# Row maximum over 16,384 rows of 1,024 floats: eight rows per partition moved to TensorE and GpSimd, fewer and larger loads, a later first store

## Chip, cores, metric

One core of a Trainium2 chip. The metric is the device time of one execution in microseconds (us). Engines in the profile: PE is TensorE (PEld its weight loads), DVE is VectorE, ACT is ScalarE, POOL is GpSimd, SP issues the loads.

## The reference

```python
x = np.random.randn(32, 512, 1024).astype(np.float32)
def reference(x):
    return np.max(x, axis=-1).astype(np.float32)
```

64 MiB are read (67.11 MB), 64 KB written. With 128 partitions that is 128 rows of 4,096 B per partition.

## The kernel before

Rows are taken in two blocks. In a block each partition owns neighbouring rows, so a load of g rows is one run of g x 4,096 B per partition. A ring of 46 rows per partition holds them; VectorE reduces each load as it lands; each block's maxima are stored when it is done.

```python
BLOCKS = [
    [14, 14, 12, 11, 9, 8, 8, 7, 6, 5, 4, 4, 4, 3, 3],
    [2, 2, 2, 2, 2, 1, 1, 1, 1, 1, 1],
]
RING = 46
# ... cut ...
        for g in loads:
            if at + g > RING:
                at = 0
            xc = ring[:, at:at + g, :]
            nc.sync.dma_start(out=xc, in_=xb[:, b:b + g, :])
            nc.vector.reduce_max(out=res[:, first + b:first + b + g], in_=xc, axis=X)
            at += g
            b += g
        # ... dst: this block's part of the output ...
        nc.scalar.dma_start(out=dst, in_=res[:, first:first + S])
```

Of the kernel before, what the change touches and what calls it, by code (L numbers as in the profile page):

```python
# [1 line left out]

# [4 lines left out]


F32 = mybir.dt.float32



BLOCKS = [
    [14, 14, 12, 11, 9, 8, 8, 7, 6, 5, 4, 4, 4, 3, 3],
    [2, 2, 2, 2, 2, 1, 1, 1, 1, 1, 1],
]
RING = 46


@with_exitstack  # L20
def kernel(
    ctx: ExitStack,
    tc: tile.TileContext,
    x: bass.AP,
    out: bass.AP,
):
    nc = tc.nc
    P = 128
    X = mybir.AxisListType.X

    xf = x.flatten_outer_dims()
    N, D = xf.shape
    I = N // P
    of = out.flatten_outer_dims()

    once = ctx.enter_context(tc.tile_pool(name="once", bufs=1))
    ring = once.tile([P, RING, D], F32)
    res = once.tile([P, I], F32)

    at = first = 0  # L40
    for loads in BLOCKS:
        S = sum(loads)
        xb = xf[first * P:(first + S) * P, :].rearrange("(p i) d -> p i d", p=P)
        b = 0
        for g in loads:
            if at + g > RING:
                at = 0
            xc = ring[:, at:at + g, :]
            nc.sync.dma_start(out=xc, in_=xb[:, b:b + g, :])  # L49
            nc.vector.reduce_max(out=res[:, first + b:first + b + g], in_=xc, axis=X)  # L50
            at += g
            b += g
        dst = bass.AP(tensor=of.tensor, offset=of.offset + first * P, ap=[[S, P], [1, S]])
        nc.scalar.dma_start(out=dst, in_=res[:, first:first + S])
        first += S
    assert first == I


# [1 line left out]
_INS = ['x']  # L60
_OUTS = [((32, 512), 'float32')]


# [23 lines left out]
```

## Time and profile before

| | before |
|---|---|
| time, median of 6 runs | 165.06 us (165.01 to 165.14) |
| span of the profiled run | 163.3 us |
| VectorE busy | 138.5 us |
| VectorE waiting for loads | 22.4 us, 20.1 of them for the first |
| last load landed / last reduction ended | 159.46 / 160.88 us |

### The profile page before, as it was taken

To read this page: it belongs to the slowest core of one execution; us is meant where nothing else is said; L and a number is where in the kernel's file an instruction comes from. 1 tells how busy PE (TensorE), PEld (TensorE's weight loads), DVE (VectorE), ACT (ScalarE), POOL (GpSimd) and SP (SyncE) were. 2 spreads that over 40 slices of the span, in tenths; PEclk is the share of its full clock that TensorE was granted. 3 is DMA by queue.
4 is the path that set the end of the run, shared out by engine and by line. 5 is a ranking of instruction groups with operands and counts; after the bars stand their busy time and mean duration, and the time that the engine had idled before them with its cause. 6 is when DMAs were issued, how large, how long until landed. Compare 5 with 4: busy or idle time off the path is not lost.

```text
span 163.3 us, 109 instructions
## 1 busy us (share of the span) xinstructions
DVE 138.5 (85%) x26; POOL 0.2 (0%) x4
## 2 busy tenths in 40 slices
DVE  0000099969999999999999999999999999999994
POOL 0000000000000000000000000000000000000000
DMA  6999999998899897999989999999999999999980
GB/s 225 449 449 449 449 449 449 449 417 385 385 409 522 353 530 321 433 433 441 473 385 473 425 449 400 434 395 451 413 425 433 429 414 418 425 421 419 404 357 2
DMA packets 4032, 67.18 MB, mean 411 GB/s; under 512 B 704, under 2 KB 704, under 8 KB 1472
## 3 DMA queue, kind: packets, MB, share of 16 engines
q1 hardware_dynamic: 3744, 67.11, 96.4%
q10 hardware_dynamic: 288, 0.07, 0.2%
HBM read 67.11 MB, written 0.07 MB: 411 GB/s over the span
## 4 chain that ended last, share of the span: by engine, by line
DMA 57%; DVE 40%; DVEq 1%; SPq 0%; issue 0%
DMA ring<-in_x_dram 57%; DVE res L50 40%; DVEq L82 1%; SPq L49 0%
## 5 line engine op out<-in xcount | busy, mean ns | idle before, releaser
L50 DVE TENSOR_REDUCE res<-ring 128x1 f32<-128x1024 f32 (+11 forms) x26 | 138.5, 5396 | 22.4 <-DMA ring<-in_x_dram 22.4
L71 POOL MEMSET const-bfloat16-1.0<- 128x1 bf16 x1 | 0.1, 101 | 0.0
L71 POOL MEMSET const-uint8-127<- 128x1 uint8 x1 | 0.1, 101 | 0.0
L71 POOL MEMSET const-float32-0.0<- 128x1 f32 x1 | 0.1, 98 | 0.2 <-issue 0.2
L71 POOL MEMSET const-float32-1.0<- 128x1 f32 x1 | 0.1, 98 | 0.0
## 6 DMA issues: line engine op xcount, KB each, us to landing
ring<-in_x_dram SPq DMA_DIRECT2D x2, 7168.0 KB, 27.6
ring<-in_x_dram SPq DMA_DIRECT2D x2, 4096.0 KB, 31.6
ring<-in_x_dram SPq DMA_DIRECT2D x1, 6144.0 KB, 49.9
ring<-in_x_dram SPq DMA_DIRECT2D x3, 2048.0 KB, 36.8
ring<-in_x_dram SPq DMA_DIRECT2D x1, 5632.0 KB, 29.7
ring<-in_x_dram SPq DMA_DIRECT2D x5, 1024.0 KB, 24.6
ring<-in_x_dram SPq DMA_DIRECT2D x1, 4608.0 KB, 23.7
ring<-in_x_dram SPq DMA_DIRECT2D x1, 3584.0 KB, 38.4
```

Of the source, the lines that this page charges most:

```text
L50: nc.vector.reduce_max(out=res[:, first + b:first + b + g], in_=xc, axis=X)
L71: nc = _bacc.Bacc("TRN2", target_bir_lowering=False, num_devices=1)
L82: with _tile.TileContext(nc) as tc:
```

## The change

Intent: eight rows per partition, out of loads that land after 120 us, take another way. TensorE turns the row block (eight turns, that is transpositions, of 128x128 into PSUM), ScalarE copies it to SBUF, GpSimd takes the maximum over partitions (the all-reduce), TensorE turns the result back, and VectorE only reduces eight numbers (the collection). The freed VectorE time is to pay for larger loads, which cost the DMA engines less. The last row comes in two halves. The first block's store goes behind the last load.

A load is now (rows, rows for GpSimd, load after which VectorE collects their result). Loads are numbered from 0.

```diff
 BLOCKS = [
-    [14, 14, 12, 11, 9, 8, 8, 7, 6, 5, 4, 4, 4, 3, 3],
-    [2, 2, 2, 2, 2, 1, 1, 1, 1, 1, 1],
+    [(15, 0, -1), (14, 0, -1), (14, 0, -1), (15, 0, -1), (15, 0, -1), (13, 0, -1), (12, 3, 7), (8, 1, 9), (6, 2, 12)],
+    [(4, 1, 14), (2, 0, -1), (2, 1, 17), (1, 0, -1), (1, 0, -1), (1, 0, -1), (1, 0, -1), (1, 0, -1), (1, 0, -1), (1, 0, -1)],
 ]
-RING = 46
+RING = 45
@@ cut @@
+    def by_gpsimd(rows, cols, m):
+        back = psmall.tile([P, m, C], F32)
+        for k in range(m):
+            ps = psum.tile([P, D], F32)
+            for c in range(C):
+                nc.tensor.transpose(out=ps[:, c * P:(c + 1) * P], in_=rows[:, k, c * P:(c + 1) * P], identity=ident)
+            sb = turn.tile([P, D], F32)
+            nc.scalar.copy(out=sb, in_=ps)
+            top = allr.tile([P, D], F32)
+            nc.gpsimd.partition_all_reduce(top, sb, P, bass_isa.ReduceOp.max)
+            run(backs)
+            def turn_back(top=top, k=k):
+                for c in range(C):
+                    nc.tensor.transpose(out=back[:, k, c:c + 1], in_=top[0:1, c * P:(c + 1) * P], identity=ident[0:1, 0:1])
+            backs.append(turn_back)
+        return lambda: nc.vector.reduce_max(out=cols, in_=back, axis=X)
@@ in the loop over loads @@
+            if m:
+                due.setdefault(w, []).append(by_gpsimd(xc[:, n - m:, :], cols[:, n - m:], m))
+            else:
+                run(backs)
+            if j == 0:
+                nc.gpsimd.tensor_copy(out=ident[:, 0:1], in_=xc[:, 0, 0:1])
+                make_identity(nc, ident)
+            if n > m:
+                reduce = nc.vector.reduce_max(out=cols[:, :n - m], in_=xc[:, :n - m, :], axis=X)
+            run(due.get(j, []))
@@ after the loop @@
+    nc.sync.dma_start(out=half, in_=xb[:, b, :H])
+    nc.sync.dma_start(out=tail[:, PAD:], in_=xb[:, b, H:])
+    nc.vector.reduce_max(out=tail[:, PAD - 1:PAD], in_=half, axis=X)
+    nc.vector.reduce_max(out=res[:, I - 1:], in_=tail[:, PAD - 1:], axis=X)
+    store = nc.scalar.dma_start(out=views[0][0], in_=views[0][1])
+    tc.add_manual_dep(store.ins, reduce.ins.name, SYNC, reason="behind the loads")
+    nc.scalar.dma_start(out=views[1][0], in_=views[1][1])
```

The next row is turned before the last one is turned back, and load 6's three results are collected after load 7's own rows, and so on.

More of the change, by code (lines that the diff above doesn't have):

```diff
@@ L6 @@
 from concourse._compat import with_exitstack
+from concourse import bass_isa
+from concourse.masks import make_identity
 F32 = mybir.dt.float32
 BLOCKS = [
-    [14, 14, 12, 11, 9, 8, 8, 7, 6, 5, 4, 4, 4, 3, 3],
-    [2, 2, 2, 2, 2, 1, 1, 1, 1, 1, 1],
-]
-RING = 46
+    [(15, 0, -1), (14, 0, -1), (14, 0, -1), (15, 0, -1), (15, 0, -1), (13, 0, -1), (12, 3, 7), (8, 1, 9), (6, 2, 12)],
+    [(4, 1, 14), (2, 0, -1), (2, 1, 17), (1, 0, -1), (1, 0, -1), (1, 0, -1), (1, 0, -1), (1, 0, -1), (1, 0, -1), (1, 0, -1)],
+]
+RING = 45
+SYNC = mybir.DependencyInfo(mybir.DependencyClass.Sync, mybir.DependencyReason.DATA)
 @with_exitstack
@@ L32 @@
     N, D = xf.shape
+    H = D // 2
+    C = D // P
     I = N // P
@@ L36 @@
     once = ctx.enter_context(tc.tile_pool(name="once", bufs=1))
+    turn = ctx.enter_context(tc.tile_pool(name="turn", bufs=2))
+    allr = ctx.enter_context(tc.tile_pool(name="allr", bufs=2))
+    psum = ctx.enter_context(tc.tile_pool(name="psum", bufs=3, space=bass.MemoryType.PSUM))
+    psmall = ctx.enter_context(tc.tile_pool(name="psmall", bufs=2, space=bass.MemoryType.PSUM))
     ring = once.tile([P, RING, D], F32)
     res = once.tile([P, I], F32)
-    at = first = 0
+    ident = once.tile([P, P], F32)
@@ new lines @@
+    PAD = 16
+    tail = once.tile([P, PAD + H], F32)
+    backs = []
+    due = {}
+    def by_gpsimd(rows, cols, m):
[3 more added lines that the diff above has]
+            for c in range(C):
+                nc.tensor.transpose(
+                    out=ps[:, c * P:(c + 1) * P],
+                    in_=rows[:, k, c * P:(c + 1) * P],
+                    identity=ident,
+                )
+            sb = turn.tile([P, D], F32)
[5 more added lines that the diff above has]
+                for c in range(C):
+                    nc.tensor.transpose(
+                        out=back[:, k, c:c + 1],
+                        in_=top[0:1, c * P:(c + 1) * P],
+                        identity=ident[0:1, 0:1],
+                    )
+            backs.append(turn_back)
+        return lambda: nc.vector.reduce_max(out=cols, in_=back, axis=X)
@@ L41, with run @@
+    def run(calls):
+        while calls:
+            calls.pop(0)()
+    at = first = j = 0
+    views = []
     for loads in BLOCKS:
-        S = sum(loads)
+        S = sum(n for n, m, w in loads) + (loads is BLOCKS[-1])
         xb = xf[first * P:(first + S) * P, :].rearrange("(p i) d -> p i d", p=P)
+        dst = bass.AP(tensor=of.tensor, offset=of.offset + first * P, ap=[[S, P], [1, S]])
+        views.append((dst, res[:, first:first + S]))
         b = 0
-        for g in loads:
-            if at + g > RING:
+        for n, m, w in loads:
+            if at + n > RING:
@@ L47 @@
                 at = 0
-            xc = ring[:, at:at + g, :]
-            nc.sync.dma_start(out=xc, in_=xb[:, b:b + g, :])
-            nc.vector.reduce_max(out=res[:, first + b:first + b + g], in_=xc, axis=X)
-            at += g
-            b += g
-        dst = bass.AP(tensor=of.tensor, offset=of.offset + first * P, ap=[[S, P], [1, S]])
-        nc.scalar.dma_start(out=dst, in_=res[:, first:first + S])
+            xc = ring[:, at:at + n, :]
+            nc.sync.dma_start(out=xc, in_=xb[:, b:b + n, :])
@@ new lines @@
+            cols = res[:, first + b:first + b + n]
+            if m:
[8 more added lines that the diff above has]
+            run(due.get(j, []))
@@ L55 @@
+            at += n
+            b += n
+            j += 1
         first += S
     assert first == I
+    half = ring[:, at, :H]
+    nc.sync.dma_start(out=half, in_=xb[:, b, :H])
[4 more added lines that the diff above has]
+    tc.add_manual_dep(store.ins, reduce.ins.name, SYNC, reason="behind the loads")
```

## The prediction

> **What bounds the kernel now.** I read the page first (busy shares, slices, queues), then the engine waits, the chain of waits, the groups by form, and a table of windows over the end.
>
> ```profile
> DVE 138.5 (85%) x26; POOL 0.2 (0%) x4
> ...
> DVE  0000099969999999999999999999999999999994
> ...
> DMA  6999999998899897999989999999999999999980
> ...
> q1 hardware_dynamic: 3744, 67.11, 96.4%
> ```
>
> Two resources are nearly full. The load queue q1 is busy for 96.4% of 163.3 us = 157.4 us, so 67.11 MB move at 426 GB/s; its digits have no hole. VectorE (DVE) is busy 138.5 us, and that is all of its time once data is there:
>
> ```profile
> DVE res L50 <- DMA ring<-in_x_dram: 22.4, 4, 20.1
> ```
>
> It waits 22.4 us in all, 20.1 of them for the first load. 22.4 + 138.5 = 160.9: its end. Which of the two ends the kernel is read in the last pieces of the chain and in the windows:
>
> ```profile
> 95.08 36.77 DMA ring<-in_x_dram
> 131.85 0.02 issue
> 131.87 19.94 DMA ring<-in_x_dram
> 151.81 0.02 issue
> 151.84 7.92 DVE res L50 x6
> 159.75 1.13 DVEq L82
> ```
>
> ```profile
> 120.00:155.00 35.00, 34.81 (x12) 0.00 (x0) 1.00 1.01 422
> 155.00:160.00 5.00, 5.00 (x6) 0.00 (x0) 1.00 0.76 304
> 160.00:163.30 3.30, 0.88 (x1) 0.00 (x0) 1.00 0.03 3
> ```
>
> The chain names VectorE for the last 8 us, but the windows show the loads at full share until about 159 (0.76 of 5 us = 3.8 us after 155). The semaphore records put the last landings at 158.21 and 159.46. The last reduction runs from 159.67 to 160.88: VectorE lags the final load by only 0.2 us. So the DMA stream is the bound and VectorE a co-bound that follows one row behind. Then the second store is issued at 160.91 and landed at 162.33 (1.42 us); the span closes 1.0 us later.
>
> ```profile
> L50 DVE TENSOR_REDUCE res<-ring 128x14 f32<-128x14336 f32 x2 | 30.2, 15086 | 22.0 <-DMA ring<-in_x_dram 22.0
> L50 DVE TENSOR_REDUCE res<-ring 128x2 f32<-128x2048 f32 x5 | 11.2, 2279 | 0.2 <-DMA ring<-in_x_dram 0.2
> L50 DVE TENSOR_REDUCE res<-ring 128x1 f32<-128x1024 f32 x6 | 6.8, 1208 | 0.0
> ```
>
> A row per partition costs VectorE 15,086 / 14 = 1.078 us in a long instruction. From two rows against one, 1.046 ns an element and 0.137 us fixed.
>
> The packet records of the trace (no view prints them; one packet is one partition of one load, eight to an engine) say what load size is worth: median 161 ns at 4,096 B, 309 at 8,192, 1,213 at 32,768, 2,116 at 57,344. The slope from 8 to 56 KB is 36.77 ns per KB of 1,000 B, with 7.8 ns fixed per packet (10.4 for the single rows). One row is 4,096 B, so 150.6 ns.
>
> **What the Trainium skill says.** "DMA: Bandwidth & Descriptors", section "Where 436 GB/s comes from", gives 435.2 GB/s as the ceiling of 16 engines. The trace agrees: 4,096 B / 150.6 ns x 16 = 435.2 GB/s before the fixed part. So nothing that reads all 67.11 MB gets below 154.2 us of stream.
> "GPSIMD Engine Reference", section 3.2 "Cross-partition", gives 247,699 ns for GpSimd's reduction over partitions of [128, 2048]. The change uses another instruction, the all-reduce, for which I find no duration on that page; the kernel before runs neither.
> "TensorE: Matmul & The Clock Gate", Part 4 "PE-mode transpose", has about 275 ns in context and 390 ns alone for a 128x128 bf16 turn; here the data is f32, and no run shows one yet.
> "ScalarE: Activation LUTs", section "What ACT_TABLE_LOAD costs", has 186 ns + 0.833 ns an element without pointer operands. That would make the 1,024-column copy 1.04 us, an estimate; the trace before has no ScalarE copy.
>
> **The change part by part.**
>
> *Larger loads.* 26 loads become 21 (19 plus two halves of the last row). Every row still costs 8 x 150.6 ns = 1.205 us, 154.2 in all. Fixed part before: 8 x (26 x 7.8 + 6 x 2.6) ns = 1.75 us; after: 8 x (21 x 7.8 + 9 x 2.6) = 1.50 us. Gain 0.25 us. This is why a large rearrangement can move so little. Five fewer completion packets of 9 ns per engine take 0.05 more.
>
> *First block's store moved.* It is 128 packets of 448 B at 25 ns, eight an engine: 0.20 us, now among the loads (issued at 142.87, loads end at 159). After, it is issued when the last loop load has been reduced, so most of it lies behind the stream. Gain 0.20 us of stream. It is ahead of the second store on the same issuing queue, by about 1.3 us, and its own issue takes some 0.4 us, so I give it 0.1 us of delay to the end.
>
> Last landing after: 159.46 - 0.25 - 0.05 - 0.20 = 158.96.
>
> *Tail.* The last whole row lands about two half rows earlier, at 157.7 (2 x 0.6 us). VectorE reduces it to 158.9 (pitch 1.125 us in the timeline, from 156.29 to 157.42), then the first half (512 elements, 0.67 us, pitch about 0.58) to 159.4, then the second half with the first's result as element 513, 0.67 us, to 160.1. Before it was 160.9. So the end moves 0.8 us, of which 0.5 is the landing and 0.3 the halved last reduction. With 0.1 for the two stores: 0.7 us.
>
> *Eight rows off VectorE.* 8 x 1.078 = 8.6 us of 138.5, less a handful of small PSUM reductions. It buys no time directly because the stream sets the end; it buys slack, so that VectorE can catch up before the last rows although bigger loads start it later (15 rows instead of 14 first: +1.2 us, to 21.3). 21.3 + 130 = 151.3, against a last loop row at 157.7: about 6 us of slack.
>
> *The new path.* Per row: eight turns (about 2.5 us, estimate from the skill's figures), a ScalarE copy (1.04), one GpSimd all-reduce T, eight small turns back (about 1.5). The rows are taken from loads 6, 7, 8, 9 and 11, which by 1.205 us a row land at 121.7, 131.4, 138.7, 143.6 and 148.5. VectorE collects the results after loads 7, 9, 12, 14 and 17, which I put at 139.0, 146.9, 151.8, 154.1 and 157.2. Three rows must fit in 17.3 us: 3T + 5.1 < 17.3, T < 4.1. From load 8 on four rows run one behind another to 157.2: 4T + 5.1 < 18.5, T < 3.35. The program fixes its collecting points unevenly, and these limits lie close together; I read that as fitted to a known T of about 3 us. That is an inference from the program, not from the trace. T below 3.35 costs nothing.
>
> **Rivals.**
> *GpSimd becomes the bound.* VectorE is in order, so a late collection stalls it. With T = 4 the last result comes 4 x 0.65 = 2.6 us late, and the end moves from -0.7 to about +1.9 us: 167.0. With T = 5 it is some 6 us over: 171. If the all-reduce behaved like the skill's partition reduction, 121 ns a column, 124 us a row, the kernel would take a millisecond. For: no duration in the profile. Against: the fitted collecting points.
> *The stream runs dry.* Load 4 (15 rows) reuses ring rows 15 to 30, which needs load 2's reduction: it lands at 55.2, ends at 70.3. Load 3's data lasts until about 73.0, and a load takes 1.0 us from issue (0.73) to first packet (1.73). The margin is 1.6 us, so no hole. If there is one, it is added whole: about +1 us. Elsewhere loads are queued by more than 10 us (before: at least 8.7 from issue to landing).
> *New traffic.* TensorE's instructions, and whatever GpSimd's all-reduce has to fetch, share the 16 engines with a stream that has no spare time. Each 0.1 us of it per engine is 0.1 us at the end. Likely some tenths; half of the gain could go, giving 164.7 to 165.1.
> *VectorE was the true bound*, as the chain says, and 8.6 us come off: 157 us. Against it: landing 159.46, 0.2 us before the last reduction. The ceiling forbids it.
>
> **Range and chances.** 165.07 - 0.7 = 164.4 as the main line. With 0.3 of new traffic it is 164.7, without and with a luckier tail 163.7; a late collection by 1 to 2 us makes 165.5 to 166.5. I state 164.5, range 163.6 to 166.0. Faster by 2% means under 161.8, which is less than stream 154.2 + start 1.7 + receipt and ramp 1.4 + a half-row reduction 0.7 + store and close 2.4 + 1.8 between span and time = 162.2: 0.01. Slower by 2% needs 168.4, so T above roughly 4.4 us or several troubles together: 0.08. Within 2%: 0.91.
>
> **What would show it.** Right: q1 still over 95% busy; windows from 20 to 155 at 425 to 432 GB/s; VectorE near 130 us busy with idle gaps of about 6 us in total before small loads, all named as waiting for loads; second store issued near 160.1; GpSimd all-reduces starting under 3.4 us apart. Wrong: a VectorE wait for TensorE's turned-back result among the last loads (GpSimd bound); a low DMA digit near 73 us (ring); loads slower than 1.205 us a row in the stage where GpSimd works (traffic or contention); or a span that starts its loads later than 0.73 us because of what the new engines set up.

## The result, and the profile after

181.52 us, median of 6 runs (181.04 to 182.66), against 165.06. The ratio is 1.100 (1.097 to 1.104): slower by 10%, 15.5 us above the top of the predicted range.

The page of the changed kernel:

```profile
PE 21.4 (12%) x128; PEld 19.4 (11%) x128; DVE 130.7 (73%) x26; ACT 9.4 (5%) x9; POOL 26.6 (15%) x15
...
DVE  0000299979995998499939999999963993387194
ACT  2000000000000000000000000000410222022000
POOL 0000000000000000000000000000793609370600
...
DMA  6999999999999999999999989999999999930000
...
q1 hardware_dynamic: 3024, 67.11, 87.7%
```

The loads end at slice 36 of 40, around 161 us, and the kernel goes on for 19 us. VectorE has holes where it had none, and GpSimd has holes between its bursts too: it is not full. VectorE's waits:

```profile
DVE res L115 <- DMA ring<-in_x_dram: 31.2, 6, 21.3
...
DVE res L86 <- PE back L79: 15.7, 4, 5.9
```

The balance closes: 31.2 + 15.7 + 130.7 = 177.6 us, VectorE's end, against 22.4 + 138.5 = 160.9 before. The 16.7 us more are 15.7 of waits for results turned back (L86 is the collection) and 8.8 of more waiting for loads, less 7.8 that came off as work. The first collection, in VectorE's timeline:

```profile
123.77 9.75 DVE L115 TENSOR_REDUCE res<-ring 128x9 f32<-128x9216 f32 x1 [0.18 <-DMA ring<-in_x_dram]
...
137.78 0.18 DVE L86 TENSOR_REDUCE res<-back 128x3 f32<-128x24 f32 x1 [4.26 <-PE back L79]
137.88 7.61 DVE L115 TENSOR_REDUCE res<-ring 128x7 f32<-128x7168 f32 x1
```

The three results of load 6 are collected *before* load 7's seven rows, which had landed at 133.46. The source has it the other way round. The chain of waits shows the second displacement:

```profile
133.38 3.31 POOL top L74
136.69 0.04 issue
136.74 1.01 PE back L79 x8
137.75 1.92 PE ps L66 x8
139.66 0.02 issue
...
139.74 1.02 ACT sb L72
140.76 0.08 issue
140.84 3.23 POOL top L74
```

TensorE turns row 3 back (136.74) and only then turns load 7's row (137.75), although the source writes load 7's turns first. So turn-back, turn, copy and all-reduce stand end to end: 7.4 us from one all-reduce to the next, of which the all-reduce is 3.25. The same pattern comes at 148.2, 158.8 and 166.2, and five whole rows and two halves are still to be reduced when the last result is there at 170.5.

The orders of the instructions, listed engine by engine, confirm it. The program builder puts instructions into an order of its own and does not keep that of the source. VectorE's collections stand before loads 7, 8 and 9, after load 10 and after load 13; the source says after loads 7, 9, 12, 14 and 17. TensorE finishes all turn-backs of a load before it turns a row of the next.

The durations themselves were as assumed or shorter:

```profile
L74 POOL PARTITION_ALL_REDUCE top<-sb x8 | 25.8, 3256 | 110.6 <-ACT sb L72 110.6
...
L72 ACT COPY sb<-ps 128x1024 f32<-128x1024 f32 x8 | 8.1, 1012 | 156.0 <-PE ps L66 154.3
```

Last, the stream. It ended at 160.83, where 158.96 was predicted and the kernel before had 159.46.

### The profile page after: what moved, and what is told of

Read it like the earlier page. It is cut to its first block, busy times and chain, and to the rows that moved or that the text cites. A ratio compares the mean times of both kernels' runs of the same rounds, so it can differ in the third digit from the quotient of the medians.

```text
span 180.0 us, 400 instructions
## 1 busy us (share of the span) xinstructions
PE 21.4 (12%) x128; PEld 19.4 (11%) x128; DVE 130.7 (73%) x26; ACT 9.4 (5%) x9; POOL 26.6 (15%) x15
## 4 chain that ended last, share of the span: by engine, by line
DMA 50%; DVE 22%; POOL 11%; PE 7%; issue 4%; ACT 2%; POOLq 2%; ACTq 0%; SPq 0%
DMA ring<-in_x_dram 50%; DVE res L115 21%; POOL top L74 11%; PE ps L66 4%; ACT sb L72 2%; PE back L79 2%; POOLq L158 2%; DVE res L127 0%; DVE tail L126 0%; ACTq L72 0%; DVE res L86 0%; SPq L104 0%
## 5 line engine op out<-in xcount | busy, mean ns | idle before, releaser
L115 DVE TENSOR_REDUCE res<-ring 128x1 f32<-128x1024 f32 (+8 forms) x19 | 129.0, 6827 | 31.2 <-DMA ring<-in_x_dram 31.2
L74 POOL PARTITION_ALL_REDUCE top<-sb x8 | 25.8, 3256 | 110.6 <-ACT sb L72 110.6
L66 PE MATMUL ps<-ident,ring 128*128 128x128 f32 x64 | 14.0, 405 | 123.9 <-DMA ring<-in_x_dram 123.9
L66 PEld LDWEIGHTS ps<-ident,ring 128*128 128x128 f32 x64 | 12.4, 218 | 123.9 <-issue 123.8
L72 ACT COPY sb<-ps 128x1024 f32<-128x1024 f32 x8 | 8.1, 1012 | 156.0 <-PE ps L66 154.3
L86 DVE TENSOR_REDUCE res<-back 128x1 f32<-128x8 f32 (+2 forms) x5 | 0.8, 169 | 15.7 <-PE back L79 15.7
L79 PE MATMUL back<-ident,top 1*128 1x1 f32 x64 | 7.7, 237 | 25.2 <-POOL top L74 25.2
L79 PEld LDWEIGHTS back<-ident,top 1*128 1x128 f32 x64 | 7.0, 204 | 27.1 <-POOL top L74 27.1
L127 DVE TENSOR_REDUCE res<-tail 128x1 f32<-128x513 f32 x1 | 0.7, 687 | 0.0
L126 DVE TENSOR_REDUCE tail<-ring 128x1 f32<-128x512 f32 x1 | 0.7, 679 | 0.0
```

The source lines that it names most:

```text
L66: nc.tensor.transpose(out=ps[:, c * P:(c + 1) * P], in_=rows[:, k, c * P:(c + 1) * P], identity=ident,)
L72: nc.scalar.copy(out=sb, in_=ps)
L74: nc.gpsimd.partition_all_reduce(top, sb, P, bass_isa.ReduceOp.max)
L79: nc.tensor.transpose(out=back[:, k, c:c + 1], in_=top[0:1, c * P:(c + 1) * P], identity=ident[0:1, 0:1],)
L86: return lambda: nc.vector.reduce_max(out=cols, in_=back, axis=X)
L115: reduce = nc.vector.reduce_max(out=cols[:, :n - m], in_=xc[:, :n - m, :], axis=X)
```

## The experiments

**Theory.** The compiled order on VectorE and TensorE makes the collections early and the all-reduces late. **Rival A:** the all-reduces themselves are the bound (8 x 3.25 us from 127 us on). **Rival B:** the later stream is what costs. The edits pin an instruction behind the one traced before it on its engine; by their intent they add no wait on another engine.

```diff
-                nc.tensor.transpose(
+                tc.keep_in_program_order(nc.tensor.transpose(      # both kinds of turns: "TensorE pinned"
-        return lambda: nc.vector.reduce_max(out=cols, in_=back, axis=X)
+        return lambda: tc.keep_in_program_order(nc.vector.reduce_max(out=cols, in_=back, axis=X))   # and the row reductions: "VectorE pinned"
```

### Both orders pinned

> The changed kernel with its turns on TensorE and its reductions on VectorE held to the order in which the source states them. My theory (the scheduler issued the collections one to two loads early and each row's turn-back ahead of the next row's turns, so VectorE idled 15.7 us on results): about 168.7 us. Worked out from the trace of the changed kernel: the three results of load 6 are collected at 141 with no idling, the turn-back of load 9's row still stands ahead of load 11's turns in the source, so the last result comes at about 162.0, VectorE ends near 164.4 and the store adds 2.4 and the launch 1.8. Rival A (the all-reduce's own 8 x 3.25 us is the bound): 180 or more, within 2 us of the changed kernel. Rival B (the load stream that ends 1.4 us later is what costs): at least 179.

169.44 us (169.01 to 170.24), ratio 1.027. 12 us come back from order alone, so rivals A and B fall as the main cause: both said at least 179. What is left of VectorE's waits for results is one of 3.54 us, for the last one. Its all-reduce starts at 158.58, after GpSimd has stood idle again:

```profile
DVE res L86 <- PE back L79: 3.5, 1, 3.5
...
158.58 3.22 POOL L74 PARTITION_ALL_REDUCE top<-sb  x1 [4.16 <-ACT sb L72]
```

The turn-back of load 9's row still stands ahead of load 11's turns, in the source itself.

### TensorE's order only

Both are pinned, but the collections are traced where the compiled changed kernel had them, so VectorE's order is exactly that of the changed kernel.

```diff
+            run(due.get(j, []))
             if n > m:
                 reduce = ...
-            run(due.get(j, []))
-(12, 3, 7), (8, 1, 9), (6, 2, 12)   (4, 1, 14)   (2, 1, 17)
+(12, 3, 7), (8, 1, 8), (6, 2, 9)    (4, 1, 11)   (2, 1, 14)
```

> Only TensorE in the source's order; VectorE's order pinned to exactly that of the changed kernel (early collections). My theory: about 173.2 us, since the first collection still stalls VectorE by 4.3 us before load 7, but the later all-reduces start about 4 us earlier each and later stalls shrink to 1 to 2 us. Rival A: 180 or more. If the early collections on VectorE were the whole cause: 179 to 181.

173.83 us (173.62 to 174.54), ratio 1.054.

### VectorE's order only

```diff
-                reduce = nc.vector.reduce_max(out=cols[:, :n - m], in_=xc[:, :n - m, :], axis=X)
+                reduce = tc.keep_in_program_order(nc.vector.reduce_max(out=cols[:, :n - m], in_=xc[:, :n - m, :], axis=X))   # and the collections
```

VectorE pinned alone; the compiled orders of the other four engines are then the same as in the changed kernel.

> Only VectorE in the source's order; TensorE, ScalarE and GpSimd exactly as in the changed kernel. My theory: about 177.2 us: the all-reduces keep their times (the last ends at 169.4), so the last result still comes at 170.5 and only one whole row and two halves follow it instead of five and two halves: 4 x 1.125 us gained. If the early collections on VectorE were the whole cause: about 166 to 169. Rival A: 177 as well, so this run alone does not tell A apart; the run with TensorE's order does.

176.67 us (176.28 to 177.49), ratio 1.071. The waits on collections, of the run with TensorE's order and then of this one:

```profile
DVE res L86 <- PE back L79: 8.4, 3, 5.2
```

```profile
DVE res L86 <- PE back L79: 11.0, 3, 5.0
```

Out of 15.7 us each order alone removes a part. TensorE's order is worth more by itself (7.7 us of time against 4.8), because it also brings the last result forward, from 170.5 to 163.3.

### Both orders, and the turn-back of load 9's row behind load 11's turns

```diff
-            else:
+            elif j != 10:
                 run(backs)
```

> Both orders, and in addition the turn-back of load 9's row put behind load 11's turns. My theory: 166.2 us: the last all-reduce starts at about 153.7, its result is there at 158, before load 17 is reduced (159.5), so VectorE follows the loads to the end: 160.8 for the last landing, 162.0 for the last reduction. About 2.5 us less than with both orders alone. If GpSimd had no spare time in the tail it would be no faster than with both orders alone.

166.22 us (165.63 to 166.85), ratio 1.007. VectorE no longer waits for a result, and GpSimd's eight all-reduces (3.25 us each, as before) fit. Around the first collection, in the timeline:

```profile
124.39 17.33 DVE L115 TENSOR_REDUCE res<-ring 128x9 f32<-128x9216 f32 x2 [0.20 <-DMA ring<-in_x_dram]
...
135.10 1.97 PE L66 MATMUL ps<-ident,ring 128*128 128x128 f32 x8
...
138.31 1.01 PE L79 MATMUL back<-ident,top 1*128 1x1 f32 x8 [1.25 <-POOL top L74]
...
141.64 0.17 DVE L86 TENSOR_REDUCE res<-back 128x3 f32<-128x24 f32 x1
```

Load 6 and load 7 are reduced back to back (17.33 us, x2). Load 7's turns run at 135.1, ahead of the turn-back at 138.3, and the collection at 141.6 waits for nothing. The 1.1 us that remain against the kernel before lie in the stream, as the next run tests. (The profiled execution was the slowest of the four, 166.85 us.)

### The same with loads 4 and 5 of 14 and 14 rows

Load 4 of 15 rows takes ring rows 15 to 29, of which row 29 is load 2's, so it is issued only when load 2 is reduced (71.1 us in the changed kernel). Below, the spread of a load is the time between the first and the last of its 16 completions, one per DMA engine.

```diff
-(15, 0, -1), (15, 0, -1), (13, 0, -1), (12, 3, 7)
+(15, 0, -1), (14, 0, -1), (14, 0, -1), (12, 3, 7)
```

> As the run with both orders and the late turn-back, with loads 4 and 5 of 14 and 14 rows instead of 15 and 13. Load 4 then reuses only load 1's rows of the ring and can be issued at about 54 instead of 71 us. If the late issue at 71 us is what makes the DMA engines fall apart (in that run the 16 completions of a load spread over 1.3 us for load 2 and 2.6 us for load 4): spread after load 4 about 1.3, stream end about 1 us earlier, 165.2 us. If the spread has another cause (the library that GpSimd fetches from 22 us on): no change, 166.2.

165.40 us (165.11 to 165.68), ratio 1.0017 (1.0004 to 1.0030). The step at load 4 is gone; a spread that arises between loads 0 and 2 stays (table below).

### No GpSimd path, the changed kernel's loads

```diff
-(12, 3, 7), (8, 1, 9), (6, 2, 12)   (4, 1, 14)   (2, 1, 17)
+(12, 0, -1), (8, 0, -1), (6, 0, -1)  (4, 0, -1)   (2, 0, -1)
-                nc.gpsimd.tensor_copy(...); make_identity(nc, ident)
```

> The changed kernel's loads, halves and late stores, but all rows on VectorE; no TensorE, ScalarE copy or GpSimd. My theory: the larger loads make VectorE wait for data about 10 us more before load 6 (waits of 1.2, 2.2, 3.3 and 2.9 us in the changed kernel), and without the eight rows taken off it cannot catch up: from load 6 at 123.7 it has 138.6 - 92.6 = 46 us left, ends at about 169.7, so 173.6 us. If larger loads cost nothing, as the prediction had it: about 165 to 167. The completions of a load should stay within 0.5 us of each other up to load 3 if the spread comes from GpSimd's library.

172.79 us (172.17 to 173.04), ratio 1.046.

```profile
DVE 138.4 (81%) x21; POOL 0.2 (0%) x4
```

```profile
DVE res L114 <- DMA ring<-in_x_dram: 30.5, 6, 21.4
```

30.5 + 138.4 = 168.9: VectorE alone cannot follow these loads. Their price is about 8 us more waiting than before (30.5 against 22.4), 1.3 of it for the first load and the rest between 38 and 93 us:

```profile
38.33 15.09 DVE L114 TENSOR_REDUCE res<-ring 128x14 f32<-128x14336 f32 x1 [0.76 <-DMA ring<-in_x_dram]
55.27 15.09 DVE L114 TENSOR_REDUCE res<-ring 128x14 f32<-128x14336 f32 x1 [1.85 <-DMA ring<-in_x_dram]
73.41 16.15 DVE L114 TENSOR_REDUCE res<-ring 128x15 f32<-128x15360 f32 x1 [3.05 <-DMA ring<-in_x_dram]
92.75 30.08 DVE L114 TENSOR_REDUCE res<-ring 128x15 f32<-128x15360 f32 x2 [3.19 <-DMA ring<-in_x_dram]
```

So the eight rows on the other path only buy back what the larger loads take. Of the descending sizes before, VectorE lost 1.85 us in this stretch.

### The same with loads of 14 and 14

```diff
-(15, 0, -1), (15, 0, -1), (13, 0, -1), (12, 0, -1)
+(15, 0, -1), (14, 0, -1), (14, 0, -1), (12, 0, -1)
```

> No GpSimd path and loads 4 and 5 of 14 and 14 rows. With the three runs before it this fills a square: late issue at 71 us (yes or no) by GpSimd's library (yes or no). If these two are the only causes of the spread of a load's 16 completions, it stays at 0.5 to 0.6 us from the first load to the last, and the stream ends at 159.3 or earlier. The time is set by VectorE, which has all rows: about 172.2 us.

172.37 us (172.19 to 172.46), ratio 1.044. The spread holds at 0.3 to 0.4 us, and the last load lands at 159.01.

### The same with the identity matrix on GpSimd

```diff
             if j == 0:
-                pass
+                nc.gpsimd.tensor_copy(out=ident[:, 0:1], in_=xc[:, 0, 0:1])
+                make_identity(nc, ident)
```

> The run before it plus only the identity matrix on GpSimd (a copy, a memset and the select with its one library, no all-reduce, no turns). If the libraries make the spread: about 1.1 us from load 1 on as in the run with the path, and no further step at load 2, because the all-reduce's library is not fetched. If the path's work on the rows makes it: 0.5 us, as without GpSimd. Time 172.2 to 173.

172.26 us (172.20 to 172.36), ratio 1.043. Spread 0.25 us throughout, so my expectation of 1.1 us failed. The reason is in GpSimd's timeline. Changed kernel first, then this one:

```profile
21.61 0.20 POOL masks.py:197 MEMSET ident<- 128x128 f32 x1
32.78 0.28 POOL masks.py:199 TENSOR_SCALAR_AFFINE_SELECT ident<-ident 128x128 f32<-128x128 f32 x1 [10.96 <-issue]
```

```profile
21.55 0.20 POOL masks.py:197 MEMSET ident<- 128x128 f32 x1
21.82 0.29 POOL masks.py:199 TENSOR_SCALAR_AFFINE_SELECT ident<-ident 128x128 f32<-128x128 f32 x1
```

The traces have a configuration instruction on GpSimd (MODIFY_POOL_CONFIG), which I take for the choice of the library that holds the code of what follows. In the changed kernel one stands at 21.87 us, 10.9 us before the select, and another at 33.31 for the all-reduces. Here the only one stands at 21.73, 0.09 us before the select. I read it so: with the all-reduce in the program two libraries alternate, and each execution waits 11 us for the select's; with the select alone its library is still there from the execution before. So this run clears the identity's instructions but says nothing of a fetch. The next one does.

### One library, all rows on the path

The run of 165.40 us with a small all-reduce in place of GpSimd's first copy, which makes the builder serve the select from the all-reduce's library: the trace has a configuration at 0.81 us and none at the select.

```diff
-                nc.gpsimd.tensor_copy(out=ident[:, 0:1], in_=xc[:, 0, 0:1])
+                nc.gpsimd.partition_all_reduce(ident[:, 0:8], xc[:, 0, 0:8], P, bass_isa.ReduceOp.max)
```

> The run with both orders, the late turn-back and loads of 14 and 14, except that GpSimd's first instruction after the first load is a small all-reduce of eight columns in place of the copy. The identity's select then runs from the same library as the all-reduces, so one library serves the whole program and stays from one execution to the next, as the select's did in the run with the identity only (0.09 us from configuration to select, against 10.9 in the changed kernel). If fetching libraries is what slows the loads: no 11 us gap on GpSimd after 22 us, the spread of a load's completions stays at 0.5 us with all eight rows still on the path, the stream ends at about 159.1, and the time is 164.3 us, below the kernel before (165.1). If the path's work itself makes the spread: 1.6 us of spread and 165.4 us as before.

165.72 us (165.60 to 165.84), ratio 1.004. The gap is gone (select at 22.44), and the spread does not move from 0.82 us while it rose to 1.66 in the run with two libraries. So changing libraries did cause that part: all six runs with two libraries rise by 0.5 to 1.1 us between loads 0 and 2, and none of the other runs does. (Load 0's 0.84 is the highest of all; whether something is fetched after the configuration at 0.81 does not show.) But the time did not come: between the landings at 148.95 and 151.31 the spread jumps to 1.85, and the stream ends at 160.10, no earlier. In that interval, from 149.13 on, the one packet of another queue keeps a DMA engine busy for 1.08 us:

```profile
q8 instruction: 1, 0.02, 0.0%
```

It is 16 KB of instructions. All runs with the path have it and none without. In the 165.40 us run it comes at 159.17, where little is left to delay. But in the changed kernel and in the run with VectorE's order it comes inside the stream too (154.96 and 155.16, 1.08 and 1.02 us long), and there the spread stays at 1.9 and 2.4. If the packet delays the engine that it meets, that was not the slowest one there; the records do not tell which it was.

The semaphore records give the spreads (us, one profiled execution each). A load counts only when the slowest engine is done.

| run | two libraries | load 4 issued late | load 0 | load 2 | load 4 | last load | last landing, us |
|---|---|---|---|---|---|---|---|
| before | no | no | 0.40 | 0.38 | 0.42 | 0.48 | 159.46 |
| no path, 14 and 14 | no | no | 0.43 | 0.40 | 0.41 | 0.29 | 159.01 |
| no path | no | yes | 0.56 | 0.52 | 1.53 | 1.33 | 160.09 |
| both orders, late turn-back, 14 and 14 | yes | no | 0.57 | 1.66 | 1.65 | 1.58 | 160.06 |
| both orders, late turn-back | yes | yes | 0.49 | 1.29 | 2.64 | 2.55 | 161.48 |
| changed kernel | yes | yes | 0.58 | 1.32 | 1.92 | 1.81 | 160.83 |
| one library, 14 and 14 | no | no | 0.84 | 0.83 | 0.82 | 1.65 | 160.10 |

In these pairs late issue and changed libraries each put about 1.1 us on the slowest engine (160.09 and 160.06 against 159.01). Together they put 1.6 to 2.5, by the five runs that have both. The size differs from run to run: with both orders pinned, the spread was 1.75 at load 2 and no larger at load 4 (1.72), though the last load still landed at 160.63.

### The store and the halves on the kernel before

First the store alone. My edit tied it to the very last reduction, later than the change does.

```diff
+    store = nc.scalar.dma_start(out=views[0][0], in_=views[0][1])      # behind both blocks
+    tc.add_manual_dep(store.ins, reduce.ins.name, SYNC, reason="behind the loads")
```

> The kernel before with only the first block's store moved behind the last load's reduction. Prediction's term: 0.2 us of stream, less up to 0.1 for the two stores in a row: 164.9 to 165.0. If the two stores in one queue cost more than the stream gains: 165.1 to 165.4.

165.41 us (165.41 to 165.66), ratio 1.0024 (1.0011 to 1.0037). The stream ends 0.2 us earlier (159.26), VectorE too, but then two stores are issued one behind the other, at 160.70 and 161.11, and the second lands at 162.63 instead of 162.33. That is the second expectation.

Then the store tied to the last whole row's reduction, as in the change, and the last row in halves:

```diff
-    [2, 2, 2, 2, 2, 1, 1, 1, 1, 1, 1],
+    [2, 2, 2, 2, 2, 1, 1, 1, 1, 1],
+    nc.sync.dma_start(out=half, in_=xb[:, b, :D // 2])
+    nc.sync.dma_start(out=tail[:, 16:], in_=xb[:, b, D // 2:])
+    nc.vector.reduce_max(out=tail[:, 15:16], in_=half, axis=X)
+    nc.vector.reduce_max(out=res[:, I - 1:], in_=tail[:, 15:], axis=X)
```

> The kernel before with the store moved and the last row loaded and reduced in two halves. Prediction's terms: 0.2 us of stream and 0.3 us of a shorter last reduction: 164.4 to 164.7. If VectorE's lag of one row at the end eats the shorter reduction: 164.9 to 165.1.

165.24 us (165.10 to 165.30), ratio 1.0007 (0.9994 to 1.0021): no gain, the first expectation fell; the second, 164.9 to 165.1, is missed by 0.1 us.

```profile
159.51 0.68 DVE L65 TENSOR_REDUCE tail<-ring 128x1 f32<-128x512 f32 x1
159.63 0.38 ACTq L67 DMA_DIRECT2D out_dram<-res  x1
160.22 0.69 DVE L66 TENSOR_REDUCE res<-tail 128x1 f32<-128x513 f32 x1
```

The halves' 0.68 and 0.69 us stand 0.71 apart, 1.40 together, against 1.21 for the whole row. VectorE was still busy with the row before when the first half landed, so it ends at 160.91, as before (160.88).

### The kernel before with a smaller start

The first two loads of 14 cut to four of 7, the store behind the last but one reduction; an attempt at a version that beats both.

```diff
-    [14, 14, 12, 11, ...
+    [7, 7, 7, 7, 12, 11, ...
```

> The kernel before with its first two loads of 14 rows cut to four of 7 and the first block's store behind the last but one reduction; no new engine. Theory: VectorE's first wait shrinks from 20.1 to about 11.6 us and its 1.4 us lag at the end goes, so the last row is reduced as it lands: 0.2 us from the store's place and 0.2 us from the lag, less 0.14 us for two more loads: 164.8 us. If the launch and the stream alone set the end: 165.1.

165.04 us (164.93 to 165.06), ratio 0.9993 (0.9981 to 1.0006): the same as the kernel before, so the expectation of 164.8 failed. VectorE's first wait fell to 11.7 us, yet its waits in all are 21.8: it waits later instead. It still starts the last row 0.2 us after its landing (159.66, 159.45), because the row before it is just being finished. No version tried is clearly faster than the kernel before.

## Why the prediction was wrong

**The step that failed** is "VectorE collects the results after loads 7, 9, 12, 14 and 17". I took the order of the source for the order of issue. The compiled order collects one to several loads earlier and puts each load's turn-backs before the next load's turns. Setting both right, and moving one more turn-back, took 181.5 to 166.2 us with the same instructions and the same durations. That is shown by four runs that were each foretold within 0.8 us.

**"Four rows run one behind another" failed as well.** T was 3.25 us, below the limit of 3.35, as I had inferred from the program. But with the source's own order (169.44 us, still 3.4 above my range) the last result came 3.54 us late: the limit takes it that the all-reduces follow each other without a gap, and GpSimd idled 4.16 us before the last, because the source puts load 9's turn-back ahead of load 11's turns. With that moved, 3.2 us came back and the limit held. A row's other parts were 1.97 us of turns, 1.01 of copy and 1.01 back, against 2.5, 1.04 and 1.5 assumed. The rival "GpSimd becomes the bound" has the sign that I named for it, VectorE waiting for a turned-back result, but not the cause: GpSimd itself stood idle for 4.16 us ahead of four of its all-reduces. The same sign has two causes, and only the engine's own idle time tells them apart.

**"About 6 us of slack" was wrong.** The sum 21.3 + 130 left out that VectorE waits between large loads, 9.9 us in the changed kernel (31.2 - 21.3). Without the path the loads give 172.8 us, where the 8.6 us of moved rows and my slack would have made VectorE late by only 2.6. With the path in order there is just enough.

**Larger loads and the store: right in size.** Without changed libraries and late issue the stream ended at 159.01, predicted 158.96. The 0.5 us was there to be had; it is not what decides.

**The halves: 0.3 us mis-sized.** The two half reductions cost 1.40 us, not the 1.25 that a pitch of 0.58 gives, and VectorE was not free when the first half landed. Store and halves together, 0.5 us in my sum, measured no gain.

**"The margin is 1.6 us, so no hole" was wrong.** Load 4 was issued at 71.1, and load 3's first engines finished at 72.9. I took the time to the first packet, 1.0 us, for the time to get going. In the trace of the kernel before the first packets of the 16 engines begin between 1.73 and 2.42, and each lasts 0.3 to 1.1 us longer than the median. The slowest engine lost about 1.1 us. My sign for it, a low DMA digit near 73 us, did not show, because the digit is a mean over 16 engines.

**"New traffic, likely some tenths" was too small.** The alternating libraries added 0.5 to 1.1 us of spread.

**What the two stream losses cost in the changed kernel** no run tests. They are not hidden: load 6 landed at 123.74, against 121.68 without them (and 121.7 predicted), and from that landing on the chain of waits goes through the row path to the end. So up to about 2 of the 16.5 us may be theirs, an estimate from these landings.

**Open:** what a change of library moves, if it is a fetch, is not in the packet records; only its effect is shown, by its absence. That the 16 KB of instructions delayed the one-library run rests on one coincidence in time and size, and why it comes at 149 in one run and between 155 and 164 in others is not known. With it out of the way that version might reach 164.7 to 164.9, an estimate: 165.72 less the 1.03 us by which the spread jumps, or the 0.83 of it that are left at the last load. It was not tried.

## What to carry to other kernels

List the compiled order of each engine before trusting a place in the source: a cheap collection issued one load early stalled VectorE until the result was there, 4.26 us the first time. When a wait names engine X, look whether X was busy or idle: GpSimd, idle for 4.16 us before four of its all-reduces, was held up by order and not by its speed. And before buying slack on an engine, add up its waits as well as its work; larger loads can take in waits what moved rows give.

## What the Trainium skill lacked or had wrong

- "GPSIMD Engine Reference", 3.2 "Cross-partition", has only the reduction of 247,699 ns for [128, 2048]. An all-reduce over partitions of [128, 1024] took 3.25 us here, of [128, 8] 0.40 us.
- "GPSIMD Engine Reference", 2.1 "Instruction dispatch", gives approximately 6 us for the first call after a library is loaded. Here it was 10.9 us from configuration to the select when two libraries alternate in every execution, and 0.1 us with the select's library alone, which the section does not mention. Nor does it say that a change of library slows running loads: with two libraries the spread of completions grew by 0.5 to 1.1 us.
- "TensorE: Matmul & The Clock Gate", Part 4, has bf16 alone (275 and 390 ns). Most groups of eight f32 turns of 128x128 took 1.97 us, 246 ns each, at a granted clock of 0.5 and of 1.0 alike.
- In no page I read: that a load issued with 1.3 to 2.5 us of work left in the queue can leave one of the 16 engines behind by about 1 us (0.4 to 1.4 us more spread in five of six runs, none in the sixth), which nothing later makes good.
- Blocks of 16 KB of instructions are described in "Runtime: NRT & Kernel Launch", "Instruction fetch mechanics", but not how long the packet of one holds a DMA engine: 0.88 to 1.43 us here, in seven runs.
